# The mixer's mask and factor products on VectorE, and the first convolution tap on ScalarE

## The chip, the cores and the metric

The kernel runs on one core of one Trainium2 chip. The metric is the device time of the whole program in microseconds. Before the change three runs took 1018.86, 1017.07 and 1013.63 us; their median is 1017.07 us.

## The reference, cut to what matters

A token block of 256 rows and 1024 columns passes through two layers with attention-like mixers and MLPs, then through a hybrid mixer, and then through 16 experts chosen by a router. The change lies in the hybrid mixer's gated delta rule:

```python
qkv = jax.nn.silu(causal_depthwise_conv(qkv, conv_w)).astype(f32)   # 4 taps
q, k, v = jnp.split(qkv, 3, axis=-1)
q = l2_normalize(to_heads(q)) * (DN_HEAD_DIM ** -0.5)
k = l2_normalize(to_heads(k))
...
# gated_delta_rule, in chunks of 64 tokens, 8 heads of 128
diff = g_cum[..., :, None] - g_cum[..., None, :]
decay = jnp.where(causal, jnp.exp(jnp.where(causal, diff, 0.0)), 0.0)
a_mat = jnp.where(strict, jnp.einsum("bnhtk,bnhsk->bnhts", k_beta, k) * decay, 0.0) + jnp.eye(DN_CHUNK)
u = solve(a_mat, v_beta)
w = solve(a_mat, k_beta * jnp.exp(g_cum)[..., None])
qk = jnp.einsum("bnhtk,bnhsk->bnhts", q, k) * decay
...
def step(state, inp):
    v_new = u_c - jnp.einsum("bhtk,bhkv->bhtv", w_c, state)
    out = jnp.einsum("bhtk,bhkv->bhtv", q_c, state) + jnp.einsum("bhts,bhsv->bhtv", qk_c, v_new)
    state = state * gl_c[..., None, None] + jnp.einsum("bhsk,bhsv->bhkv", k_c, v_new)
```

Behind it stand a spatial gating unit, gates, an output projection, the router (top group, then two experts of it) and the experts.

## The kernel before

The program is written as calls on recorders, one for each engine (V for VectorE, S for ScalarE, G for GpSimd, PE, SP). Nothing is issued while it is recorded. A planner, the class Plan, gives each operation an estimated cost by engine and size (`_cost`, L163 to 192) and each hand-over between engines a price (a table at L30), and then decides in `order` the order on every engine, the place of every DMA on SP's queue, and the buffers: H is a pool of 47 blocks in SBUF, P the eight PSUM banks. Where it foresees TensorE idle it puts in filler matmuls of k_ones (L589). So an operation that changes its engine lets the planner order everything behind it anew. In the trace all recorded operations have line L594.

The stages in order are an attention layer, an MLP, a gated linear attention layer, an MLP, the hybrid mixer and the experts. In the trace the mixer begins at about 555 us. Its parts that matter here:

`qkv(hg)` (L1374), run for two groups of four heads. For q, k and v and for each pair of 128 features, projection matmuls fill one PSUM bank of banks 5 to 7 (H<-P,s_cw in the rows reads them as P); then the causal convolution goes over the bank in four taps: the first writes an accumulator (L1388), three more add to it shifted by one to three tokens (255, 254 and 253 elements in the rows). A tanh on ScalarE and a product on VectorE follow. There are 24 first taps, two to a bank.

`solve(hg, i)` (L1406), run for two head groups and two halves of the tokens, builds the chunk matrices, 128 x 256 each (four heads, two chunks of 64). E is an exponential of a matmul's result on ScalarE, masked with c_incl (L1430). From the squares of k and q come eight columns of factors (the tile hp; the power function runs on GpSimd). Ew is E times a factor (L1448), U is Ew times the product of keys (L1457), E is then scaled by another factor (L1458). kde, read from a PSUM bank with another factor, lets that bank go. L is a copy of U turned by matmuls, N its inverse in the making: five levels (L1478) each take L times a level mask, Lm (L1480), two sets of small matmuls, a copy on ScalarE and a subtraction on VectorE. The five Lm of a solve depend on L alone.

`recur(hg)` (L1499) then steps the state through the chunks. The mixer runs qkv(0), both solves of group 0 in turns, qkv(1), the first solve of group 1 together with recur(0), the second solve, and recur(1). The spatial gating unit's matmuls, 128 x 512, take their banks from 6 and 7 and are laid between.

VectorE also makes the "splits": `SCALAR_TENSOR_TENSOR H<-H,H 128x512 f16`, which write the low half of a weight or activation that goes into TensorE as two f16 parts.

Of the kernel before, what the change touches and what calls it, by code (L numbers as in the profile page):

```python
# [11 lines left out]
AF = mybir.ActivationFunctionType  # L12
OP = mybir.AluOpType
# [592 lines left out]
def block_kernel(ctx: ExitStack, tc: tile.TileContext, I: dict, out: bass.AP, dbg=None, stop=None):  # L606
    nc = tc.nc
    plan = Plan(nc)
    V, S, G, PE, SP = plan.DVE, plan.ACT, plan.POOL, plan.PE, plan.SP
# [13 lines left out]
    def PS(name, banks, dtype=F32):  # L623
        return plan.tile([128, 512 if dtype == F32 else 1024], name, dtype, "P", banks, psum=True)
# [4 lines left out]
    def A(shape, name, dtype=F32):  # L629
        return plan.tile(shape, name, dtype, "H", None)  # L630
# [4 lines left out]
    def B(shape, name, dtype=F32):  # L635
        return plan.tile(shape, name, dtype, "H", None)

    def C(shape, name, dtype=F32):
        return plan.tile(shape, name, dtype, "H", None)

    def sm(shape, name, dtype=F32, bufs=2):
        return plan.tile(shape, name, dtype, "s_" + name, bufs)
# [4 lines left out]
    def h4v(ap, n=4):  # L647
        return ap.rearrange("p (h t) -> p h t", h=n)

    def bc_free(col, n):  # L650
        return col[:, :, None].to_broadcast([col.shape[0], col.shape[1], n])

    def bc_mid(m, n):
        return m[:, None, :].to_broadcast([m.shape[0], n, m.shape[1]])
# [54 lines left out]
    def load_k8(src, c0, n, name):  # L709
        return [load_unit([(src[512 * u:512 * (u + 1), c0:c0 + n], 0)], 4, n, f"{name}{u}") for u in range(2)]  # L710
# [13 lines left out]
    def formB(po, us, c0, c1, xt, ts=slice(0, 256)):  # L724
        kt = 4 * len(us)
        for u, w in enumerate(us):
            for k in range(4):
                kk = 4 * u + k
                wh, wl = w.at(0, k, slice(c0, c1)), w.at(1, k, slice(c0, c1))
                xh, xl = tok(xt.h, kk, ts), tok(xt.l, kk, ts)  # L730
                o = like(po, xh)
                PE.matmul(o, wh, xh, start=(kk == 0), stop=False)
                PE.matmul(o, wh, xl, start=False, stop=False)
                PE.matmul(o, wl, xh, start=False, stop=(kk == kt - 1))
# [583 lines left out]
    def mixer(x, xt, then=None):  # L1318
# [8 lines left out]
        cw = sm([128, 96], "cw", bufs=1)  # L1327
# [46 lines left out]
        def qkv(hg):  # L1374
            res = []
            for r in range(3):
                us = load_k8(win, 1024 * r + 512 * hg, 512, f"d{r}")
                fT = A([128, 4, 256], f"dT{r}")
                for m in range(2):
                    p = PS("pqkv", (5, 6, 7))  # L1380
                    for mm in range(2):
                        c0 = 128 * (2 * m + mm)
                        formB(p[:, 256 * mm:256 * (mm + 1)], us, c0, c0 + 128, xt)
                    ac = C([128, 2, 256], "cacc")
                    for mm in range(2):
                        ft = 8 * r + 4 * hg + 2 * m + mm
                        pm = p[:, 256 * mm:256 * (mm + 1)]
                        V.tensor_scalar(ac[:, mm], pm, cw[:, 72 + ft:73 + ft], None, op0=OP.mult)  # L1388
                        for sh in range(1, 4):
                            tp = 24 * (3 - sh) + ft  # L1390
                            V.scalar_tensor_tensor(out=ac[:, mm, sh:], in0=pm[:, 0:256 - sh], scalar=cw[:, tp:tp + 1],
                                                   in1=ac[:, mm, sh:], op0=OP.mult, op1=OP.add)
                    th = C([128, 2, 256], "cth")
                    S.activation(th, ac, AF.Tanh, scale=0.5)
                    V.scalar_tensor_tensor(out=fT[:, 2 * m:2 * m + 2], in0=th, scalar=1.0, in1=ac, op0=OP.add, op1=OP.mult)
                res.append(fT)
            return res
# [8 lines left out]
        def solve(hg, i, qT, kT, vT):  # L1406
# [4 lines left out]
            def quads(p, lhs, rhs, width=64, c0=0):  # L1411
                for h4 in range(4):
                    for e in range(2):
                        PE.matmul(p[R[e], c0 + width * h4:c0 + width * (h4 + 1)], lhs[R[e], h4],
                                  rhs[R[e], h4] if len(rhs.shape) == 3 else rhs[R[e]], start=True, stop=True, skip_group_check=True)
# [11 lines left out]
            quads(p, gm, c_inclf)  # L1427
            E = B([128, 4, 64], "E")
            S.activation(E, h4v(p[:, 0:256]), AF.Exp)
            G.tensor_tensor(E, E, bc_mid(c_incl, 4), op=OP.mult)  # L1430
            yield
            w = sm([128, 10, 4], "hp", bufs=4)
            pt = {}
# [11 lines left out]
            V.tensor_tensor(w[:, 5], be[i][:, hs], rk, op=OP.mult)  # L1445
            V.tensor_tensor(w[:, 6], w[:, 5], rk, op=OP.mult)
            Ew = B([128, 4, 64], "Ew")
            G.tensor_tensor(Ew, E, bc_free(w[:, 6], 64), op=OP.mult)  # L1448
            V.tensor_tensor(w[:, 7], eg[i][:, 1, hs], rk, op=OP.mult)
            V.scalar_tensor_tensor(out=w[:, 4], in0=w[:, 1], scalar=0.5, in1=rk, op0=OP.mult, op1=OP.mult)  # L1450
            V.tensor_scalar(w[:, 8], eg[i][:, 0, hs], -1.0, None, op0=OP.mult)
# [3 lines left out]
            own(pk, kT, kT)  # L1455
            U = B([128, 4, 64], "U")
            V.tensor_tensor(U, h4v(pk[:, 0:256]), Ew, op=OP.mult)  # L1457
            G.tensor_tensor(E, E, bc_free(w[:, 3], 64), op=OP.mult)  # L1458
            pl = PS("pL", banks)
            quads(pl, U, c_id)  # L1460
            L = B([128, 4, 64], "L")
# [15 lines left out]
            yield  # L1477
            for lv in range(1, 6):  # L1478
                Lm = B([128, 4, 64], "Lm")
                G.tensor_tensor(Lm, L, bc_mid(lev[:, lv], 4), op=OP.mult)  # L1480
                pt_ = PS("pT", banks)
                quads(pt_, Lm, N)
                Tm = B([128, 4, 64], "Tm")
                S.activation(Tm, h4v(pt_[:, 0:256]), AF.Copy)
                pn = PS("pN", banks)
                quads(pn, NT, Tm)
                if lv < 5:
                    quads(pn, Tm, NT, c0=256)
                    V.tensor_tensor(NN.rearrange("p a h t -> p (a h t)"), NN.rearrange("p a h t -> p (a h t)"), pn, op=OP.subtract)
                else:  # L1490
                    V.tensor_tensor(N, N, h4v(pn[:, 0:256]), op=OP.subtract)
                yield
# [69 lines left out]

        z_gate(1)
        t0 = qkv(0)
        together(solve(0, 0, *t0), solve(0, 1, *t0))
        t1 = qkv(1)
        together(solve(1, 0, *t1), recur(0))
        together(solve(1, 1, *t1))
        together(recur(1))

# [78 lines left out]
        for c in range(2):  # L1649
            gated(tdn[c], "w_dn_out_2", c, oT, "wd")  # L1650
            for m in range(2):
# [5 lines left out]
                                       op0=OP.mult, op1=OP.subtract)  # L1657
# [462 lines left out]
```

## Time and profile before

| | us |
|---|---|
| median of three runs | 1017.07 |
| the profiled execution, own time | 1020.56 |
| its span, first to last instruction | 1018.9 |
| TensorE busy | 983.1 (96%) |
| VectorE busy | 810.9 (80%) |
| ScalarE busy | 582.2 (57%) |
| GpSimd busy | 78.5 (8%) |
| mean granted TensorE clock | 0.982 of full speed |

The profile gives busy times of each engine over the span or over a stretch, and lists of instructions with the idle time ahead of them and the engine that ended it. Instructions on one engine overlap by some tens of nanoseconds, so a group's busy time can be less than its count times its mean. A clock of 1.00 is 2.4 GHz, 0.50 is 1.2 GHz.

### The profile page before, as it was taken

What the parts mean: (1) busy time and instruction counts of PE and PEld (TensorE: products, weight loads), DVE (VectorE), ACT (ScalarE), POOL (GpSimd) and SP (SyncE); (2) the same over time, 40 slices, a digit from 0 to 9 for tenths busy, and PEclk for the clock granted to TensorE, in tenths of its full rate; (3) what the DMA queues carried; (4) which work ended last, traced back from release to release, by engine and by line L of the source; (5) the groups of instructions that cost most, each with busy time, mean ns of one, the idle gap of its engine ahead of it and who ended that gap; (6) DMA issues with size and microseconds to landing.
All of it is one profiled execution on the core that took longest, in us unless ns stands there. A gap on an engine that the chain in (4) does not pass through costs nothing. (4 is left out here: it accounts for less than half of the span.)

```text
span 1018.9 us, 22293 instructions
## 1 busy us (share of the span) xinstructions
PE 983.1 (96%) x8760; PEld 680.2 (67%) x8760; DVE 810.9 (80%) x1654; ACT 582.2 (57%) x1180; POOL 78.5 (8%) x121
## 2 busy tenths in 40 slices
PE   9999999999999999999999999989999999989994
PEld 8875777668458557766675787846788889553431
DVE  7899986656868898665659998958865688999985
ACT  7796555556448655555555752425543376568670
POOL 3000000000000000000001305003110000110000
PEclk9899999999999999999999999989899999999997
DMA  9927795676462467566867954414436676659992
GB/s 347 374 87 241 242 348 169 207 247 194 159 227 67 145 220 256 196 208 206 204 174 150 213 131 104 126 42 84 145 65 203 224 257 207 226 188 365 364 359 93
DMA packets 123009, 205.38 MB, mean 202 GB/s; under 512 B 7553, under 2 KB 43137, under 8 KB 122898
## 3 DMA queue, kind: packets, MB, share of 16 engines
q1 hardware_dynamic: 122898, 203.90, 64.7%
q8 instruction: 70, 1.15, 0.4%
q14 instruction: 41, 0.34, 0.1%
HBM read 202.82 MB, written 1.05 MB: 200 GB/s over the span
## 5 line engine op out<-in xcount | busy, mean ns | idle before, releaser
L594 PE MATMUL P<-H,H 128*128 128x256 f16 (+10 forms) x7736 | 918.8, 298 | 14.5 <-DVE H L594 6.7
L594 PEld LDWEIGHTS <-H 128*128 128x128 f16 (+3 forms) x6456 | 549.3, 99 | 261.6 <-issue 41.3
L594 ACT ACTIVATE H<-H 128x512 f16<-128x512 f32 (+2 forms) x777 | 443.9, 621 | 212.8 <-PE P L594 107.1
L594 DVE SCALAR_TENSOR_TENSOR H<-H,H 128x512 f16<-128x512 f32 (+2 forms) x715 | 456.4, 684 | 51.1 <-ACT H L594 48.9
L594 ACT ACTIVATE H<-P 128x256 f32<-128x256 f32 (+7 forms) x247 | 119.4, 497 | 190.3 <-PE P L594 181.2
L594 PEld LDWEIGHTS P<-H,H 64*64 64x64 f32 (+4 forms) x1424 | 67.7, 136 | 35.7 <-issue 23.0
L594 DVE TENSOR_TENSOR H<-H 128x512 f32<-128x512 f32 (+6 forms) x44 | 31.2, 709 | 44.2 <-ACT H L594 44.2
L594 POOL TENSOR_TENSOR s_bnr<-s_bnr,k_mhalf 128x1 f32<-128x1 f32 x14 | 13.4, 960 | 602.6 <-DVE s_bnr L594 602.6
L594 DVE SCALAR_TENSOR_TENSOR H<-P,H 128x512 f32<-128x512 f32 (+2 forms) x56 | 37.7, 684 | 20.0 <-PE P L594 11.7
L594 PE MATMUL P<-k_ident,H 128*128 128x128 f32 x256 | 46.1, 285 | 3.6 <-DVE H L594 2.6
L594 DVE TENSOR_TENSOR H<-H,H 128x512 f16<-128x512 f32 (+6 forms) x50 | 34.3, 694 | 10.2 <-ACT H L594 9.9
L594 PEld LDWEIGHTS P<-k_ident,H 128*128 128x128 f32 x256 | 31.9, 145 | 14.1 <-DVE H L594 5.6
L594 DVE TENSOR_TENSOR H<-H,P 128x512 f32<-128x512 f32 (+1 forms) x32 | 19.6, 613 | 13.7 <-PE P L594 13.6
L594 DVE SCALAR_TENSOR_TENSOR H<-P,s_cw,H 128x255 f32<-128x255 f32 (+2 forms) x72 | 29.7, 470 | 0.0
L594 DVE TENSOR_TENSOR H<-P,H 128x512 f16<-128x512 f32 (+2 forms) x38 | 23.5, 640 | 4.0 <-ACT H L594 4.0
L594 DVE SCALAR_TENSOR_TENSOR H<-H,s_bnr,H 128x512 f32<-128x512 f32 x28 | 21.2, 790 | 0.0
L594 DVE BATCH_NORM_STATS2 s_bns<-H 128x6 f32<-128x512 f32 x28 | 19.0, 683 | 1.8 <-ACT H L594 1.6
L594 DVE SCALAR_TENSOR_TENSOR H<-H,s_bnm,H 128x512 f32<-128x512 f32 x28 | 19.8, 741 | 0.0
L594 DVE SCALAR_TENSOR_TENSOR H<-H,P 128x512 f32<-128x512 f32 (+1 forms) x24 | 14.3, 594 | 6.0 <-ACT H L594 3.0
L594 PE MATMUL P<-H 128*64 128x64 f32 (+6 forms) x200 | 17.9, 255 | 0.7 <-DVE H L594 0.6
L589 PE MATMUL P<-k_ones 128*128 128x128 f16 x194 | 15.7, 235 | 1.1 <-DVE k_ones L594 1.1
L594 DVE TENSOR_TENSOR H<-P,s_hp 128x512 f32<-128x512 f32 (+1 forms) x16 | 10.9, 684 | 7.0 <-PE P L594 6.6
(220 smaller groups left out, 345.7 us busy)
## 6 DMA issues: line engine op xcount, KB each, us to landing
H<-in_mlp_w_dram SPq DMA_DIRECT2D x128, 512.0 KB, 4.9
H<-in_w_in_dram SPq DMA_DIRECT2D x64, 512.0 KB, 5.6
H<-in_expert_w_gate_dram SPq DMA_DIRECT2D x64, 256.0 KB, 5.9
H<-in_expert_w_up_dram SPq DMA_DIRECT2D x64, 256.0 KB, 5.9
H<-in_expert_w_down_dram SPq DMA_DIRECT2D x32, 512.0 KB, 7.0
H<-in_c_w_in_dram SPq DMA_DIRECT2D x24, 512.0 KB, 4.4
H<-in_a_w_in_dram SPq DMA_DIRECT2D x12, 512.0 KB, 8.1
H<-in_a_w_out_dram SPq DMA_DIRECT2D x8, 512.0 KB, 10.7
```

The costliest lines, as they stand in the source:

```text
L589: tc.nc.tensor.matmul(self.phys["P", ~i][:, 0:128], ap, ap, start=True, stop=True)
L594: fn(*[self._place(a) if isinstance(a, bass.AP) else a for a in args], **{k: self._place(a) if isinstance(a, bass.AP) else a for k, a in k ...
```

## The change

Four products of `solve` are given to VectorE instead of GpSimd: the causal mask of E, the factor products Ew and E, and the level masks Lm, 4 + 4 + 4 + 20 = 32 instructions of 128x256. The first tap of the convolution is given to ScalarE as a copy with a column as scale, instead of VectorE: 24 instructions of 128x256, read from PSUM.

```diff
-                        V.tensor_scalar(ac[:, mm], pm, cw[:, 72 + ft:73 + ft], None, op0=OP.mult)
+                        S.activation(ac[:, mm], pm, AF.Copy, scale=cw[:, 72 + ft:73 + ft])
...
-            G.tensor_tensor(E, E, bc_mid(c_incl, 4), op=OP.mult)
+            V.tensor_tensor(E, E, bc_mid(c_incl, 4), op=OP.mult)
...
-            G.tensor_tensor(Ew, E, bc_free(w[:, 6], 64), op=OP.mult)
+            V.tensor_tensor(Ew, E, bc_free(w[:, 6], 64), op=OP.mult)
...
-            G.tensor_tensor(E, E, bc_free(w[:, 3], 64), op=OP.mult)
+            V.tensor_tensor(E, E, bc_free(w[:, 3], 64), op=OP.mult)
...
-                G.tensor_tensor(Lm, L, bc_mid(lev[:, lv], 4), op=OP.mult)
+                V.tensor_tensor(Lm, L, bc_mid(lev[:, lv], 4), op=OP.mult)
```

The planner itself is unchanged, and up to the front of the mixer the order is the same on all engines. From there it differs. The number of real matmuls stays; the fillers go from 194 to 220.

First place, GpSimd and VectorE at the first head group's solves. The names: H are blocks, k_lev the level masks, P_115 bank 5 with a filled projection. GpSimd's rows before, from the first causal mask to the last level mask of the two solves:

```order
L594 TENSOR_TENSOR H_100<-H_100,k_c_incl_124 128x256 x2
L594 TENSOR_TENSOR s_hp_196<-s_hp_196,k_mhalf_137 128x8
L594 TENSOR_TENSOR H_89<-H_100,s_hp_196 128x256
L594 TENSOR_TENSOR H_100<-H_100,s_hp_196 128x256
L594 TENSOR_TENSOR s_hp_197<-s_hp_197,k_mhalf_137 128x8
L594 TENSOR_TENSOR H_89<-H_100,s_hp_197 128x256
L594 TENSOR_TENSOR H_100<-H_100,s_hp_197 128x256
L594 TENSOR_TENSOR H_109<-H_75,k_lev_132 128x256 x4
L594 TENSOR_TENSOR H_74<-H_75,k_lev_132 128x256 x4
L594 TENSOR_TENSOR H_83<-H_75,k_lev_132 128x256
L594 TENSOR_TENSOR H_75<-H_75,k_lev_132 128x256
```

VectorE after the change, the ten level masks and the taps on bank 5 behind them:

```order
L594 TENSOR_TENSOR H_109<-H_95,k_lev_132 128x256 x4
L594 TENSOR_TENSOR H_100<-H_100,P_113 128x256
L594 TENSOR_TENSOR H_74<-H_95,k_lev_132 128x256 x2
L594 TENSOR_TENSOR H_109<-H_95,k_lev_132 128x256
L594 TENSOR_TENSOR H_74<-H_95,k_lev_132 128x256
L594 TENSOR_TENSOR H_109<-H_95,k_lev_132 128x256
L594 TENSOR_TENSOR H_100<-H_100,P_111 128x256
L594 SCALAR_TENSOR_TENSOR H_105<-P_115,s_cw_163,H_105 128x255 x2
L594 TENSOR_TENSOR H_79<-H_95,k_lev_132 128x256
L594 SCALAR_TENSOR_TENSOR H_105<-P_115,s_cw_163,H_105 128x254 x2
L594 SCALAR_TENSOR_TENSOR H_105<-P_115,s_cw_163,H_105 128x253 x2
```

The masks have moved from GpSimd's queue to VectorE's, nine of them ahead of bank 5's accumulating taps. A little earlier on VectorE, Ew, E and U now stand ahead of kde, which stood ahead of U.

Second place, VectorE at the end of qkv(1): the last taps of the convolution, on bank 6 (P_116), which the spatial unit's matmuls use next. Before:

```order
L594 SCALAR_TENSOR_TENSOR H_103<-H_71,H_103 128x512 x2
L594 TENSOR_SCALAR H_83<-P_116,s_cw_163 128x256 x2
L594 SCALAR_TENSOR_TENSOR H_83<-P_116,s_cw_163,H_83 128x255 x2
L594 SCALAR_TENSOR_TENSOR H_83<-P_116,s_cw_163,H_83 128x254 x2
L594 TENSOR_TENSOR H_108<-H_108,P_113 128x512
L594 SCALAR_TENSOR_TENSOR H_83<-P_116,s_cw_163,H_83 128x253 x2
L594 TENSOR_TENSOR H_82<-P_117,k_m_full_134 128x512
```

After:

```order
L594 SCALAR_TENSOR_TENSOR H_86<-H_76,H_86 128x512
L594 SCALAR_TENSOR_TENSOR H_105<-P_116,s_cw_163,H_105 128x255 x2
L594 TENSOR_TENSOR H_95<-H_95,P_112 128x512
L594 SCALAR_TENSOR_TENSOR H_105<-P_116,s_cw_163,H_105 128x254 x2
L594 TENSOR_TENSOR H_67<-H_67,P_110 128x512
L594 SCALAR_TENSOR_TENSOR H_105<-P_116,s_cw_163,H_105 128x253 x2
L594 TENSOR_TENSOR H_109<-P_117,k_m_full_134 128x512
```

The pair of first taps is gone from VectorE, and two subtractions of the solves stand between the accumulating taps where one stood. ScalarE now makes the two first taps of a bank one behind the other, and VectorE's first accumulating tap waits for the second of them.

Third place, VectorE at the last factors (s_hp_199) of the first solves of group 1. Before:

```order
L594 TENSOR_TENSOR H_106<-k_c_id_123,H_106 128x256
L594 SCALAR_TENSOR_TENSOR H_79<-H_70,H_79 128x512 x2
L594 TENSOR_TENSOR s_hp_199<-s_db_168,s_hp_199 128x4
L594 TENSOR_TENSOR s_hp_199<-s_eg_178,s_hp_199 128x4
L594 SCALAR_TENSOR_TENSOR s_hp_199<-s_hp_199 128x4
L594 TENSOR_TENSOR s_hp_199<-s_hp_199 128x4
L594 TENSOR_SCALAR s_hp_199<-s_hp_199 128x4
```

After:

```order
L594 TENSOR_TENSOR H_89<-H_81,k_lev_132 128x256
L594 SCALAR_TENSOR_TENSOR H_108<-P_114,s_hp_197,H_108 64x128 x3
L594 TENSOR_TENSOR H_95<-H_100,P_113 128x512
L594 SCALAR_TENSOR_TENSOR H_108<-P_114,s_hp_197,H_108 64x128
L594 TENSOR_TENSOR H_103<-P_111,s_eg_178 64x512
L594 TENSOR_TENSOR H_100<-H_81,k_lev_132 128x256
L594 TENSOR_TENSOR H_108<-H_81,k_lev_132 128x256 x2
L594 SCALAR_TENSOR_TENSOR s_onm_222<-s_onm_222 128x4
L594 TENSOR_TENSOR s_hp_199<-s_db_168,s_hp_199 128x4
L594 TENSOR_SCALAR s_onm_222<-s_onm_222 128x4
L594 TENSOR_TENSOR s_hp_199<-s_eg_178,s_hp_199 128x4
```

Level masks (one more stands two rows above these) are now between and ahead of the factor steps, where before they stood on GpSimd.

On SP's queue two expert tiles, four DMAs of 256 KB, are issued ahead of the last projection weights of the mixer; three more expert units than before have been issued when the router's flag is made. In the router's chain on VectorE six splits of 128x512 now stand among the steps of the first token tile.

## Rows read from the trace of the kernel before

**Rows 1.** The page's first part: busy time, share of the span and instructions.

```profile
PE 983.1 (96%) x8760; PEld 680.2 (67%) x8760; DVE 810.9 (80%) x1654; ACT 582.2 (57%) x1180; POOL 78.5 (8%) x121
```

**Rows 2.** Stretches: us, busy of PE, PEld, DVE, ACT, POOL, clock, DMA share, GB/s.

```profile
560.00:600.00 40.00, 40.00 (x365) 31.36 (x363) 37.48 (x81) 24.55 (x46) 8.68 (x4) 1.00 0.79 185
600.00:620.00 20.00, 17.29 (x192) 14.59 (x190) 18.19 (x49) 9.18 (x42) 8.16 (x7) 0.94 0.79 160
620.00:640.00 20.00, 19.52 (x296) 16.57 (x294) 18.58 (x39) 7.62 (x15) 8.45 (x12) 0.98 0.14 45
640.00:660.00 20.00, 19.31 (x301) 16.38 (x300) 19.86 (x43) 8.49 (x17) 0.00 (x0) 1.00 0.42 131
660.00:680.00 20.00, 17.18 (x146) 9.04 (x141) 10.57 (x21) 5.06 (x9) 0.00 (x0) 0.83 0.17 56
...
700.00:720.00 20.00, 17.24 (x207) 13.87 (x207) 17.77 (x45) 9.35 (x27) 7.99 (x8) 1.00 0.28 65
720.00:740.00 20.00, 19.73 (x218) 15.40 (x219) 17.12 (x37) 10.94 (x25) 2.71 (x4) 0.83 0.57 171
```

**Rows 3.** Timeline of TensorE: start, us, instruction, count, [idle ahead, what ended it].

```profile
616.41 0.44 PE L594 MATMUL P<-k_ident,H 128*128 128x128 f32 x2 [1.27 <-DVE H L594]
617.26 0.51 PE L594 MATMUL P<-k_c_id,H 64*64 64x64 f32 x8 [0.42 <-DVE H L594]
...
666.24 2.29 PE L594 MATMUL P<-H,H 128*128 128x512 f16 x5 [2.25 <-DVE H L594]
...
707.65 1.60 PE L594 MATMUL P<-H,H 128*64 128x128 f32 x21 [1.39 <-DVE H L594]
...
719.87 2.74 PE L594 MATMUL P<-H,H 128*64 128x128 f32 x16 [1.37 <-DVE H L594]
```

**Rows 4.** VectorE's groups by form, 555 to 760 us: busy us, mean ns | idle.

```profile
L594 DVE TENSOR_SCALAR H<-P,s_cw 128x256 f32<-128x256 f32 x24 | 10.5, 474 | 0.2
...
L594 DVE TENSOR_TENSOR H<-k_c_id,H 128x256 f32<-128x256 f32 x8 | 4.4, 563 | 0.1
...
L594 DVE TENSOR_TENSOR H<-H,k_lev1t 128x256 f32<-128x256 f32 x4 | 1.7, 413 | 0.0
```

**Rows 5.** ScalarE's groups by form, 555 to 760 us.

```profile
L594 ACT ACTIVATE H<-P 128x256 f32<-128x256 f32 x24 | 8.6, 376 | 28.1 <-PE P L594 26.6 <-DVE s_hp L594 1.2
```

**Rows 6.** Timeline of VectorE at the end of qkv(1).

```profile
659.38 3.09 DVE L594 SCALAR_TENSOR_TENSOR H<-H,H 128x512 f16<-128x512 f32 x5
662.39 0.87 DVE L594 TENSOR_SCALAR H<-P,s_cw 128x256 f32<-128x256 f32 x2
```

**Rows 7.** GpSimd's groups by form, 555 to 760 us.

```profile
L594 POOL TENSOR_TENSOR H<-H,k_lev 128x256 f32<-128x256 f32 x20 | 14.1, 736 | 15.5 <-DVE H L594 13.5 <-ACT H L594 1.9
...
L594 POOL TENSOR_TENSOR H<-H,s_hp 128x256 f32<-128x256 f32 x8 | 5.1, 636 | 2.1 <-DVE s_hp L594 1.7
L594 POOL TENSOR_TENSOR H<-H,k_c_incl 128x256 f32<-128x256 f32 x4 | 3.4, 840 | 30.2 <-ACT H L594 30.1
```

**Rows 8.** Timelines of VectorE, then GpSimd, in the first chunk.

```profile
615.67 0.68 DVE L594 TENSOR_TENSOR H<-P,s_hp 128x512 f32<-128x512 f32 x1
...
616.80 0.41 DVE L594 TENSOR_TENSOR H<-P,H 128x256 f32<-128x256 f32 x1
617.13 0.67 DVE L594 TENSOR_TENSOR H<-P,s_hp 128x512 f32<-128x512 f32 x1
...
615.85 1.30 POOL L594 TENSOR_TENSOR H<-H,s_hp 128x256 f32<-128x256 f32 x2 [0.58 <-DVE s_hp L594]
```

**Rows 9.** Timelines of VectorE, then GpSimd, at the fourth chunk's factors.

```profile
704.11 0.62 DVE L594 TENSOR_TENSOR s_hp<-s_db,s_hp 128x4 f32<-128x4 f32 x1 [0.27 <-POOL s_hp L594]
704.66 0.15 DVE L594 TENSOR_TENSOR s_hp<-s_eg,s_hp 128x4 f32<-128x4 f32 x1
...
704.04 2.55 POOL L594 TENSOR_TENSOR H<-H,k_lev 128x256 f32<-128x256 f32 x4
```

**Rows 10.** One stretch of the experts, columns as in rows 2.

```profile
906.00:996.00 90.00, 85.68 (x796) 36.41 (x790) 82.50 (x153) 69.51 (x134) 0.00 (x0) 1.00 1.06 354
```

## The prediction

> **What bounds the kernel now.** I read the page's totals first [rows 1]: TensorE is busy 983.1 of 1018.9 us, VectorE 810.9, GpSimd 78.5. A kernel that is 96% TensorE can gain only where TensorE stands still or is clocked down, so the next view is the table of stretches [rows 2], kept to the mixer's chunk work, the only place that the change touches. Before 600 us TensorE is busy all 40.00 of 40.00 us: nothing is to be had there. Between 600 and 740 the six rows shown leave TensorE 2.71 + 0.48 + 0.69 + 2.82 + 2.76 + 0.27 = 9.7 us idle. The clock column is read with it: 0.94, 0.98, 0.83 and 0.83 of full speed in four of those rows, so 20 x (0.06 + 0.02 + 0.17 + 0.17) = 8.4 us are lost to the lower of the two levels (1.2 GHz instead of 2.4). All that an edit here can win is thus about 18 us, and only if every gap closes.
>
> Third view: who ended TensorE's gaps. The list of its matmuls [rows 3] shows four gaps over 1 us, all ended by VectorE: 1.27 us until 616.41 (and 0.42 until 617.26), 2.25 until 666.24, 1.39 until 707.65, 1.37 until 719.87. The clock falls behind the first, the second and the last, not behind 707.65. VectorE is the engine to watch: in 600 to 660 it is 18.2 to 19.9 us busy in each 20 [rows 2], while in 660 to 680 it works 10.57 us. So VectorE is nearly full up to about 667, and has room after.
>
> **Part 1, the taps.** Removed from VectorE: 24 first taps, 10.5 us [rows 4]. Added to ScalarE: 24 copies of 128x256 from PSUM with a column as scale. The nearest row is ScalarE's plain copy out of PSUM of the same shape, 376 ns [rows 5]: 24 x 0.376 = 9.0 us. ScalarE is busy 24.55 of the 40 us before 600 and 7.6 to 9.2 us of each 20 up to 640 [rows 2], so that work lies beside other work. From below, the two taps of a bank may overlap and cost less than 0.376 each; from above, a tap as long as VectorE's, 474 ns, gives 11.4 us. I take 9.0, the row of the same engine and shape.
>
> The bank's latency does not get shorter, however. Before, a bank was emptied by one engine: a pair of taps took 0.87 us, then the other taps followed at once [rows 6]. After, by the order, ScalarE makes both taps and VectorE's first accumulating tap waits for the second: 2 x 0.376 = 0.75 us plus a hop between engines, and ahead of it whatever ScalarE has in hand. So a bank is freed no earlier unless VectorE was the one that was late; where VectorE's queue is the delay, it is earlier by the 0.87 us that left the queue.
>
> A sentence of the Trainium skill speaks against this part: "ScalarE: Activation LUTs", section "What ACT_TABLE_LOAD costs", has a pointer operand (here the scale column) add about 93 ns to an activation; no row here shows one with such a scale on this shape. By it the taps would cost an estimated 24 x 0.093 = 2.2 us more of ScalarE's time, still beside other work.
>
> **Part 2, the 32 products.** GpSimd gives up 20 level masks, 14.1 us, 8 factor products, 5.1, and 4 causal masks, 3.4 [rows 7]: 22.6 us. VectorE takes 32 products of 128x256 with both operands in SBUF; its own of that kind takes 413 ns [rows 4], and the start of the next instruction comes 0.33 us after such a product (617.13 after 616.80 [rows 8]). So 32 x 0.33 to 32 x 0.413 = 10.6 to 13.2 us are added. That is about what the taps gave back.
>
> What also goes is interference. VectorE's subtraction from the identity has two SBUF operands as well and should cost 413 ns; it took 563 on average [rows 4], 8 x 0.15 = 1.2 us; GpSimd's masks run in the same stretches. At 704.11 a 128x4 step took 0.62 us, the next 0.15, while GpSimd made four masks from 704.04 on [rows 9]; there are three such slow steps within 2 us, 3 x 0.47 = 1.4 us, just ahead of the gap that ended at 707.65. So at least 2.6 us of VectorE time come back.
>
> VectorE's account up to 667: minus 10.5 for the taps, plus 16 products, 5.3 to 6.6, minus about 1: **5 to 6 us lighter**, in the stretch where it is full. After 667: plus 5.3 to 6.6, minus 1.6: **4 to 5 us heavier**, where it idles more than that.
>
> **Where it reaches TensorE.** (a) The first chunk, gap until 617.26. Before: factor on VectorE, then GpSimd makes Ew and E from 615.85 on, 1.30 us for two, then U on VectorE at 616.80 [rows 8]. After, Ew, E and U stand one behind another on VectorE: 615.85 and two steps of 0.33 put U at 616.5, 0.3 us earlier. But in the new order kde, which at 615.67 released TensorE's transposes at 616.41, stands behind U, about 1 us later. I count 0, bounds -0.7 and +1 us.
>
> (b) The gap of 2.25 us until 666.24. The first spatial matmul needs the bank that qkv(1)'s last taps empty; VectorE came to them at 662.39, after five splits, 3.09 us from 659.38 [rows 6]. In the new order the pair of taps is gone and VectorE has 5 to 6 us less behind it, but two subtractions of the solve now stand between the accumulating taps where one stood. I take **-2 us**: the gap shrinks to a few tenths. Bounds: 0 (TensorE feeds those taps itself, so its earlier end only moves the gap) and -2.25 and the whole 3.4 us of lost clock, -5.7.
>
> (c) The gap of 1.39 us until 707.65. The slowed steps, 1.4 us, go. Five level masks now stand on VectorE just ahead of the same steps, 5 x 0.33 = 1.7 us. I take **-0.5**, since some of them fall into idle time; bounds -1.4 and +1.7.
>
> (d) 719.87: VectorE's own splits ended that gap; no term, bounds -1.4 and +1.4.
>
> (e) The clock. I let half of one of the two drops of 3.4 us go: **-1.5**, bounds -6.8 and +3.4.
>
> (f) The tail. From 906 to 996 the DMA share is 1.06 at 354 GB/s [rows 10]: the expert weights set the end. In the new order three more 0.26-MB units are issued before the router's flag, 3 x 0.26 MB / 354 GB/s = 2.2 us off; against that, six weight splits of 0.62 us (3.09 / 5 [rows 6]) now stand in the router's chain on VectorE for the first tokens, 3.7 us on. They are missing later, so I take **+0.5**, bounds -2.2 and +3.7.
>
> Sum: 0 - 2 - 0.5 + 0 - 1.5 + 0.5 = **-3.5 us**, so 1017.1 us by the profiled execution (1020.6). That one lay 3.5 us above the median of the three runs (1017.1), so the forecast is 1017.1 - 3.5 = **1013.6 us**.
>
> **Rivals.** *VectorE was the whole cause.* With 5 to 6 us less in its queue up to 667, the gaps at 616 and 666 close (1.69 and 2.25 us) with their clock, 1.6 + 3.4: -8.9, and with the 1.4 at 707 -10.3: about **1007 us**, down to 1002 if 719.87 and its 3.4 go too. For it: all four gaps end on VectorE [rows 3]. Against it: the solve is a chain of small steps through TensorE, ScalarE and VectorE, and of the moved products only the causal mask and Ew stand in it, since the level masks are made ahead of their use.
>
> *Nothing reaches TensorE.* 96% busy, the masks were off its path, the gain at 666 appears again at the next hand-over: **1017 us**, 1015 to 1020. For it: TensorE is full before 600, and GpSimd's slowness nowhere ended a gap of TensorE directly [rows 3].
>
> *The masks block the bank (slower).* In the new order ten level masks of the first two chunks stand almost together on VectorE, 10 x 0.33 = 3.3 us, ahead of the accumulating taps on bank 5; before, GpSimd made them beside it, 10 x 0.7 = 7 us [rows 7]. If TensorE has less than about 2 us of other work at that place, a gap over 1.3 us opens, of the size that brought the lower clock behind three of four gaps: up to 3.3 + 3.4 = 6.7 us, **1023.8 us**. It decides from the point where bank 6 and bank 7 are full too. A rule of the Trainium skill makes this sharper ("PSUM — Partial Sum Buffer", section "PSUM bank collisions raise a hardware error"): two engines may not read one bank at once. By it ScalarE's taps can't run beside VectorE's, so the bank waits for both engines in turn; the order shows that wait, the trace of before none.
>
> **How the numbers follow.** Chances: forecast 0.42 (own range 1010 to 1018), whole cause 0.22, nothing 0.18, masks block 0.18. The measurement tells 0.5%, 5.1 us, from no change, so the bounds are 1012.0 and 1022.2. Faster: 0.20 of the second and 0.16 of the forecast's lower end, 0.36. Slower: 0.16 of the last. Same: 0.48. The range runs from the middle of the second case to the last one's value: 1004 to 1024, leaving out about 0.1 below and 0.1 above.
>
> **What would show it.** Right: VectorE's busy time in 600 to 667 falls by 4 to 7 us; the gap at the first spatial matmul is under 0.6 us; the identity subtraction falls to about 415 ns; ScalarE's tap costs 0.35 to 0.5 us; TensorE's busy time is unchanged and no new gap over 1.3 us appears between 600 and 760. Wrong: a gap over 1.3 us at bank 5's taps, with the clock at half behind it; the gap at the first spatial matmul still 2 us, with VectorE idle before it; or the end set by the router's chain, seen as expert weights landing later against the router's flag.

## The result and the profile after

The changed kernel takes 1012.30 us, the median of nine runs (1010.94 to 1013.66), against 1017.07 for nine runs of the kernel before. The ratio is 0.9947, with a 95% interval of 0.9933 to 0.9961: 0.5% faster, 4.8 us by the medians. The forecast was 1013.6.

| | before | after |
|---|---|---|
| median of nine runs, us | 1017.07 | 1012.30 |
| the profiled execution, own time, us | 1020.56 | 1011.38 |
| its span, us | 1018.9 | 1009.6 |
| its mean granted TensorE clock | 0.982 | 0.988 |

The page's first part after the change, which answers to [rows 1]:

```profile
PE 977.2 (97%) x8786; PEld 679.7 (67%) x8786; DVE 804.2 (80%) x1662; ACT 591.9 (59%) x1204; POOL 55.5 (5%) x89
```

GpSimd lost 23 us of work and ScalarE gained 10, which is about what the moved instructions take. VectorE is 6.7 us lighter in sum. The stretches, which answer to [rows 2] (us, busy of PE, PEld, DVE, ACT and POOL, clock, DMA share, GB/s), and the same two stretches up to and behind the mixer's first spatial matmul:

```profile
600.00:620.00 20.00, 18.03 (x246) 15.59 (x244) 16.20 (x50) 9.55 (x44) 3.29 (x2) 1.00 0.69 173
620.00:640.00 20.00, 20.00 (x312) 17.13 (x311) 17.02 (x41) 6.87 (x15) 0.00 (x0) 1.00 0.08 26
640.00:660.00 20.00, 19.12 (x316) 16.44 (x314) 19.29 (x38) 12.64 (x27) 0.00 (x0) 1.00 0.25 75
660.00:680.00 20.00, 19.76 (x181) 11.87 (x182) 9.41 (x19) 9.94 (x25) 0.93 (x1) 1.00 0.27 88
...
700.00:720.00 20.00, 19.70 (x252) 16.08 (x251) 19.54 (x46) 11.64 (x25) 1.97 (x2) 1.00 0.68 151
720.00:740.00 20.00, 17.85 (x273) 15.26 (x271) 14.40 (x31) 9.69 (x20) 0.00 (x0) 0.91 0.37 107
...
600.00:667.00 67.00, 63.98 (x929) 53.01 (x927) 55.57 (x132) 31.66 (x89) 3.29 (x2) 1.00 0.36 100
667.00:760.00 93.00, 90.14 (x1092) 69.18 (x1090) 74.04 (x171) 49.29 (x123) 8.02 (x6) 0.98 0.32 86
```

The two last stretches in the kernel before:

```profile
600.00:667.00 67.00, 60.36 (x859) 50.82 (x857) 63.64 (x142) 27.46 (x78) 16.61 (x18) 0.96 0.46 117
667.00:760.00 93.00, 89.65 (x966) 64.42 (x965) 65.18 (x141) 43.76 (x112) 19.27 (x22) 0.94 0.33 81
```

TensorE's idle time from 600 to 760 us is 160 less its busy time: 9.99 us before, 5.88 after. That sum is used for every experiment below. VectorE is 8.1 us lighter up to 667 and 8.9 heavier behind it.

The gaps of TensorE that are left, answering to [rows 3] (start, us, instruction, count, [idle ahead, what ended it]):

```profile
610.02 0.66 PE L594 MATMUL P<-k_ident,H 128*128 128x128 f32 x4 [1.47 <-ACT H L594]
...
613.62 0.56 PE L594 MATMUL P<-k_c_id,H 64*64 64x64 f32 x12 [0.22 <-DVE H L594]
...
658.79 0.68 PE L594 MATMUL P<-H,H 64*64 64x64 f32 x16 [0.73 <-DVE H L594]
...
660.16 0.45 PE L594 MATMUL P<-H,H 64*64 64x64 f32 x8 [0.31 <-DVE H L594]
...
704.47 1.75 PE L594 MATMUL P<-H,H 128*64 128x128 f32 x15 [0.21 <-DVE H L594]
...
727.21 0.68 PE L594 MATMUL P<-H,H 64*64 64x64 f32 x16 [2.15 <-DVE H L594]
```

Why the two profiled executions differ by 9.2 us and the medians by 4.8: the runs of one kernel do not all get the same clock. In a series of 30 runs of the kernel before, the mean clock lay between 0.982 and 0.991 with a median of 0.988, and the time between 1022.2 and 1014.1. The profiled execution of before had 0.982, as low as the lowest of them. The nine runs after had 0.985 to 0.989, median 0.987. So the clock's 8.4 us that [rows 2] shows lost were mostly that one execution's bad luck, and the medians hold no such part. Over all runs of this study a thousandth of clock goes with about 0.7 us; at one clock of 0.988 that makes, from the means of the 30 and of the nine runs, an estimated 1017.0 us before and 1011.7 after.

In the profiled pair, from the start of VectorE's first accumulating tap to its first step on the router's logits the time fell from 304.95 to 294.90 us (-10.05: about 4.1 of idle time and 6.6 of clock, less 0.45 of added fillers). From there to the start of VectorE's last instruction it rose from 129.24 to 131.71 us (+2.5), and the first accumulating tap came 1.8 us earlier, about 1.0 of which arose in work that the change leaves alone.

### The profile page after: what moved, and what is told of

It reads as the page before. It is cut to its first block, busy times and chain, and to the rows that moved or that the text cites. A ratio compares the mean times of both kernels' runs of the same rounds, so it can differ in the third digit from the quotient of the medians.

```text
span 1009.6 us, 22338 instructions
## 1 busy us (share of the span) xinstructions
PE 977.2 (97%) x8786; PEld 679.7 (67%) x8786; DVE 804.2 (80%) x1662; ACT 591.9 (59%) x1204; POOL 55.5 (5%) x89
## 5 line engine op out<-in xcount | busy, mean ns | idle before, releaser
L594 PE MATMUL P<-H,H 128*128 128x256 f16 (+8 forms) x7780 | 914.7, 297 | 10.4 <-DVE H L594 6.0
L594 PEld LDWEIGHTS <-H 128*128 128x128 f16 (+2 forms) x6456 | 547.5, 99 | 255.8 <-issue 35.9
L594 PEld LDWEIGHTS P<-H,H 64*64 64x64 f32 (+4 forms) x1472 | 70.1, 138 | 33.2 <-issue 18.8
L589 PE MATMUL P<-k_ones 128*128 128x128 f16 x220 | 18.9, 247 | 2.6 <-ACT H L594 1.5
L589 PEld LDWEIGHTS <-k_ones 128*128 128x128 f16 x220 | 16.5, 114 | 2.7 <-issue 1.3
```

Source lines behind the costliest of these rows:

```text
L589: tc.nc.tensor.matmul(self.phys["P", ~i][:, 0:128], ap, ap, start=True, stop=True)
L594: fn(*[self._place(a) if isinstance(a, bass.AP) else a for a in args], **{k: self._place(a) if isinstance(a, bass.AP) else a for k, a in k ...
```

## The experiments

The planner orders everything behind a change of engine anew, so an edit changes two things at once: which engine does the work, and the order on all engines. The first eight experiments take these apart. `plan.add` names the engine for which the planner reckons and places an operation, and separately the function that is issued. With the two set apart, TensorE's and SP's orders stay row for row those of one kernel, while the engines are those of another.

**Both parts, in the order of before.**

```diff
-                        V.tensor_scalar(ac[:, mm], pm, cw[:, 72 + ft:73 + ft], None, op0=OP.mult)
+                        plan.add("DVE", "tensor_scalar", nc.scalar.activation, (ac[:, mm], pm, AF.Copy), dict(scale=cw[:, 72 + ft:73 + ft]))
...
-                G.tensor_tensor(Lm, L, bc_mid(lev[:, lv], 4), op=OP.mult)
+                plan.add("POOL", "tensor_tensor", nc.vector.tensor_tensor, (Lm, L, bc_mid(lev[:, lv], 4)), dict(op=OP.mult))
...
```

The other three products are edited like Lm.

> The planner plans as for the kernel before (taps costed and placed as VectorE's, products as GpSimd's), so TensorE's and SP's orders are those of before, row by row; only the engine that executes the taps (ScalarE) and the 32 products (VectorE) is that of the changed kernel. Theory A, the engines did it (VectorE's queue is lighter up to 667 us, and GpSimd's interference is gone): 1012 to 1014 us, and the identity subtraction falls to about 420 ns. Theory B, the new order did it: 1017 us or above, since the old order now has products in places that were planned for GpSimd.

Measured: 1023.62 us, ratio 1.0058 (1.0037 to 1.0079). The very engines of the changed kernel make the program 0.6% slower in the old order. VectorE's accumulating taps show a part of the reason (group by form, 555 to 765 us: busy, mean ns | idle ahead, releaser):

```profile
L594 DVE SCALAR_TENSOR_TENSOR H<-P,s_cw,H 128x255 f32<-128x255 f32 x24 | 10.6, 477 | 10.8 <-ACT H L594 10.8
...
L594 DVE TENSOR_TENSOR H<-k_c_id,H 128x256 f32<-128x256 f32 x8 | 3.3, 420 | 0.1
```

VectorE waits 10.8 us for ScalarE's first taps. At the end of qkv(1) one sees it happen (ScalarE, then VectorE, then TensorE):

```profile
667.67 0.47 ACT L594 ACTIVATE H<-P,s_cw 128x256 f32<-128x256 f32 x1
...
668.17 1.65 DVE L594 SCALAR_TENSOR_TENSOR H<-P,s_cw,H 128x255 f32<-128x255 f32 x4 [1.61 <-ACT H L594]
...
671.26 2.27 PE L594 MATMUL P<-H,H 128*128 128x512 f16 x7 [3.17 <-DVE H L594]
```

ScalarE reaches the second tap behind other work of its own queue, VectorE stands 1.61 us, and the first spatial matmul's gap is 3.17 us instead of 2.25. The identity subtraction is at 420 ns, so the interference with GpSimd is gone here too, and yet the kernel is slower.

**Both parts undone, in the order of after.** The mirror image: planned as S and V, issued on VectorE and GpSimd.

```diff
-                        S.activation(ac[:, mm], pm, AF.Copy, scale=cw[:, 72 + ft:73 + ft])
+                        plan.add("ACT", "activation", nc.vector.tensor_scalar, (ac[:, mm], pm, cw[:, 72 + ft:73 + ft], None), dict(op0=OP.mult))
...
-                V.tensor_tensor(Lm, L, bc_mid(lev[:, lv], 4), op=OP.mult)
+                plan.add("DVE", "tensor_tensor", nc.gpsimd.tensor_tensor, (Lm, L, bc_mid(lev[:, lv], 4)), dict(op=OP.mult))
...
```

> The mirror image: planned as the changed kernel, with its orders of TensorE and SP, but the taps run on VectorE and the 32 products on GpSimd, as before the change. Theory A: 1016 to 1019 us, with the identity subtraction back above 500 ns and VectorE's gaps ahead of TensorE back. Theory B: 1012 to 1013 us.

Measured: 1019.76 us, ratio 1.0010 (0.9996 to 1.0025). The new order by itself is worth nothing. TensorE's largest gap lies in the first chunk:

```profile
612.83 1.12 PE L594 MATMUL P<-k_ident,H 128*128 128x128 f32 x4 [3.74 <-ACT H L594]
```

At 606.80 in this run VectorE still had the last bank's two taps ahead of their accumulation (0.86 us), so the tanh behind them began on ScalarE at 610.09, and the squares, for which TensorE's transposes wait, came behind that tanh. So neither theory held: the engines alone lose 0.6%, the order alone gives 0, both together win 0.5%.

**Each part alone, in the order of before.** The tap's line of the first diff alone, then the products' lines alone.

> TensorE's and SP's orders of the kernel before, products on GpSimd as before; only the 24 first taps run on ScalarE, in the places that were planned for VectorE. Theory A (engine speed) would have this faster than before, 1014 us. Theory C, drawn from the first four runs: in the old order ScalarE reaches a tap late, behind a tanh that waits for VectorE, so VectorE waits for taps (10.8 us of waiting in the run with both parts); the loss of that run, about 5 us at equal clock, is the taps': 1020 to 1023 us.

> TensorE's and SP's orders of the kernel before, taps on VectorE as before; only the 32 products run on VectorE, in the places planned for GpSimd. Theory C: VectorE is some 5 us heavier up to 667 us but the interference of about 1 us goes there and 1.6 us later: within 2 us of before, 1016 to 1019 us. If the loss of the run with both parts came from the products in places not planned for them: 1020 to 1023 us.

Measured: tap alone 1020.81 us, 1.0027 (1.0013 to 1.0042); products alone 1020.09 us, 1.0024 (1.0010 to 1.0038). The tap's loss is the wait named above; VectorE's first accumulating taps of this run:

```profile
L594 DVE SCALAR_TENSOR_TENSOR H<-P,s_cw,H 128x255 f32<-128x255 f32 x24 | 10.5, 477 | 11.5 <-ACT H L594 11.5
```

The losses add up to about that of both, 0.3 + 0.2 against 0.6%. I had put all of it on the taps; nearly half of it is the products'. With them alone on VectorE TensorE's three gaps in the first chunk are 1.70 + 1.28 + 1.02 us, where they were 1.03 + 1.27 + 0.42; that VectorE's longer queue is the reason there is inferred, not shown.

**Each part undone alone, in the order of after.** The tap's line of the second diff alone, then the products' lines alone.

> TensorE's and SP's orders of the changed kernel, its products on VectorE; only the taps are back on VectorE, in the places planned for ScalarE. VectorE then carries both, 10.5 us more up to 667 us. Theory C: the gaps of 3.7 us in the first chunk and 2.6 us at the first spatial matmul, which the run with both parts undone showed, are the taps': 1016 to 1019 us. If the products made the gain: 1012 to 1013 us.

> TensorE's and SP's orders of the changed kernel, its taps on ScalarE; only the 32 products are back on GpSimd. Theory C: the interference comes back (the identity subtraction near 490 ns or above) and the products' 0.65 to 0.85 us replace 0.42, 2 to 3 us of which reach TensorE: 1013 to 1015 us. If the products made the gain: 1016 to 1018 us.

Measured: with the taps back on VectorE 1023.23 us, 1.0059 (1.0038 to 1.0079); with the products back on GpSimd **1012.25 us, 0.9943 (0.9923 to 0.9963)**, the same as the changed kernel. Both lie outside what I expected of theory C, 1016 to 1019 and 1013 to 1015 us. The second is the run that settles the most. In the new order the tap is everything: it is worth 0.7% where the products are on GpSimd (1.0010 to 0.9943), and 1.1% where they are on VectorE (1.0059 to 0.9947). Part of both is a lower clock, a median of 0.981 in the run with the taps back and 0.9835 in the one with both parts back; by the means, at one clock of 0.988 and 0.7 us for a thousandth, the tap is worth an estimated 5.5 and 7.3 us. That lower clock is not the luck of single executions: all seven with the taps back got 0.980 to 0.983, while 25 of the kernel before, timed beside them, got 0.983 to 0.990. So part of the clock belongs to the kernel and not to the execution; what in the kernel sets it, these runs do not show.

The products' change of engine is worth nothing that these runs resolve (intervals of about 2 us to either side), though the interference is back. The identity subtraction (VectorE by form, 555 to 765 us), first after the change, then with the products back on GpSimd:

```profile
L594 DVE TENSOR_TENSOR H<-k_c_id,H 128x256 f32<-128x256 f32 x8 | 3.4, 421 | 0.0
```

```profile
L594 DVE TENSOR_TENSOR H<-k_c_id,H 128x256 f32<-128x256 f32 x8 | 4.0, 499 | 0.1
```

563 ns before [rows 4], 421 after, 499 with the masks on GpSimd again: the interference is real, and in this order it does not show in the time. The Trainium skill states the cause ("SBUF — State Buffer", section "Who interferes with whom"): a VectorE instruction with two inputs in SBUF shares a read port with GpSimd's reads. The trace agrees, 563 and 499 ns against 421. The page's first part for the run with the products back shows what it all weighs:

```profile
PE 976.6 (97%) x8786; PEld 679.8 (67%) x8786; DVE 796.3 (79%) x1630; ACT 592.0 (59%) x1204; POOL 76.3 (8%) x121
```

VectorE is busy 796.3 us there and 804.2 in the changed kernel. The 32 products cost it 12.4 us (below), so about 4.5 us of interference were saved in return, and 7.9 us more is what the move leaves on VectorE.

**Each part alone, planned anew.** The tap's line or the products' lines of the change itself.

> Only the first tap goes to ScalarE; the products stay on GpSimd; planned anew. Theory A gives the larger part of the gain to the taps, since they take 10.5 us from VectorE up to 667 us: 1013 to 1015 us. A rival, that the products and the interference are the cause: 1017 us. If the new order alone decides, anything between 1010 and 1020.

> Only the 32 products go to VectorE; the taps stay there too; planned anew. Theory A: VectorE is 5 to 6 us heavier up to 667 us and only some 1 us of interference comes back there, so the gap ahead of the first spatial matmul grows: 1018 to 1021 us. The rival, that the interference and GpSimd's slowness were the cause: 1012 to 1014 us.

Measured: tap alone 1015.34 us, 0.9974 (0.9957 to 0.9992); products alone 1017.71 us, 1.0007 (0.9988 to 1.0026). As expected the tap carries a gain and the products none, though both times lie just outside the ranges given, 1013 to 1015 and 1018 to 1021 us. But the run with the tap alone has exactly the engines of the run with the products back, at 1012.25 us: 3 us lie between two orders of the same work. In the slower of the two, TensorE's largest gap, and VectorE in front of it:

```profile
653.65 5.50 DVE L594 SCALAR_TENSOR_TENSOR H<-H,H 128x512 f16<-128x512 f32 x9
659.40 1.26 DVE L594 SCALAR_TENSOR_TENSOR H<-P,s_cw,H 128x255 f32<-128x255 f32 x3 [0.24 <-ACT H L594]
660.58 0.68 DVE L594 TENSOR_TENSOR H<-H,P 128x512 f32<-128x512 f32 x1
...
661.40 1.12 PE L594 MATMUL P<-H,H 64*64 64x64 f32 x16 [2.71 <-DVE H L594]
```

Nine splits, 5.50 us, stand on VectorE ahead of a solve's subtraction (660.58) for which TensorE waits 2.71 us. The changed kernel has eight splits at that place, 5.00 us, but from 652.31 us on, and its gap there is 0.73. The gap that the changed kernel has left, 2.15 us until 727.21, is of the same kind, with six splits in front:

```profile
722.60 3.70 DVE L594 SCALAR_TENSOR_TENSOR H<-H,H 128x512 f16<-128x512 f32 x6
726.21 0.35 DVE L594 SCALAR_TENSOR_TENSOR H<-H,s_onm,H 128x128 f32<-128x128 f32 x1
726.47 0.69 DVE L594 TENSOR_TENSOR H<-H,P 128x512 f32<-128x512 f32 x1
```

**Other orders by other prices.** The last four change a price in the planner, and so the order, of four sets of engines. The line behind an operation sets its estimated cost, here that of the tap:

```diff
                         S.activation(ac[:, mm], pm, AF.Copy, scale=cw[:, 72 + ft:73 + ft])
+                        plan.ops[-1] = plan.ops[-1][:4] + (465.0,) + plan.ops[-1][5:]
```

The products on GpSimd get 736.0 in the same way. First the engines of before, then tap on ScalarE with the products on GpSimd at the new price:

> The engines of the kernel before, all of them; only the price that the planner has for the 32 products on GpSimd is changed, from 658 to 736 ns, the mean that the trace of before shows for the level masks. It shows what a new order alone does with unchanged engines. Theory C (the engines matter only through the order that is planned for them, and orders differ by chance): anywhere within 5 us of before, 1012 to 1022 us. If the planner's wrong price was what held the old order back: 1013 us or less.

> Taps on ScalarE, products on GpSimd, planned anew with the products at 736 instead of 658 ns. These are the engines of the run with the tap alone (1015.3 us) and of the run in the changed kernel's order with the products back (1012.3 us). If the tap's gain is robust against the order: 1012 to 1016 us. If it is an accident of one order: anything up to 1020 us.

Then the changed kernel with the tap at its measured price, and tap and products on GpSimd with both prices:

> The changed kernel with one price of the planner put right: the tap on ScalarE at 465 ns, as the trace after the change shows it, instead of 265. Engines as in the changed kernel. If the fit of the plan to the engines is what counts, VectorE's waits for the tap (2.1 us) shrink: 1010 to 1012 us. If orders scatter by chance: 1010 to 1018 us.

> Taps on ScalarE at the price of 465 ns, products on GpSimd at 736 ns: both prices as the traces show them, the products left where they were before the change. If the products' move is worth nothing and the price of the tap counts: 1010 to 1013 us, as fast as the changed kernel or faster. If orders scatter by chance: 1010 to 1018 us.

Measured: engines of before 1020.67 us, 1.0027 (1.0009 to 1.0045); tap with a new price for the products 1015.39, 0.9969 (0.9952 to 0.9987); tap with both prices 1016.12, 0.9986 (0.9971 to 1.0002); and the changed kernel with the tap's price put right **1009.13, 0.9920 (0.9894 to 0.9946)**, the fastest of all. Its largest gap of TensorE between 600 and 760 us is 0.55 us:

```profile
600.00:667.00 67.00, 65.99 (x935) 53.80 (x933) 53.86 (x126) 29.21 (x84) 3.30 (x2) 1.00 0.37 104
667.00:760.00 93.00, 90.91 (x1090) 69.75 (x1089) 68.90 (x161) 44.65 (x115) 8.85 (x6) 1.00 0.32 86
```

```profile
L594 DVE SCALAR_TENSOR_TENSOR H<-P,s_cw,H 128x255 f32<-128x255 f32 x24 | 10.5, 476 | 1.1 <-ACT H L594 0.9
```

VectorE's wait for taps fell to 1.1 us from the 2.1 of the changed kernel, and TensorE's idle time to 3.1 us. The same group in the changed kernel:

```profile
L594 DVE SCALAR_TENSOR_TENSOR H<-P,s_cw,H 128x255 f32<-128x255 f32 x24 | 10.5, 480 | 2.1 <-ACT H L594 2.1
```

A truer price did not always help, however. The products' price put right made the engines of before 3.6 us slower, where 1013 us or less was expected if the wrong price had held the old order back; with the tap on ScalarE it changed nothing (1015.34 to 1015.39 us); and the tap's price put right beside it changed nothing for the better (1015.39 to 1016.12), where 1010 to 1013 was expected if that price counted. Only with the products on VectorE did it gain 3 us. So these four runs do not tell a better fit from orders that scatter by some microseconds. All runs side by side, with that idle time (160 us less TensorE's busy time in the two stretches); each experiment's ratio is to runs of the kernel before timed in its own series, whose medians were 1017.26, 1017.38 and 1017.13 us:

| taps on | products on | order | idle, us | median, us | ratio |
|---|---|---|---|---|---|
| VectorE | GpSimd | own (before) | 9.99 | 1017.07 | 1 |
| VectorE | GpSimd | own, products' price 736 | 11.2 | 1020.67 | 1.0027 |
| VectorE | GpSimd | of after | 9.8 | 1019.76 | 1.0010 |
| VectorE | VectorE | own | 10.5 | 1017.71 | 1.0007 |
| VectorE | VectorE | of before | 12.7 | 1020.09 | 1.0024 |
| VectorE | VectorE | of after | 11.2 | 1023.23 | 1.0059 |
| ScalarE | GpSimd | own | 8.6 | 1015.34 | 0.9974 |
| ScalarE | GpSimd | own, products' price 736 | 7.0 | 1015.39 | 0.9969 |
| ScalarE | GpSimd | own, both prices | 8.2 | 1016.12 | 0.9986 |
| ScalarE | GpSimd | of before | 13.5 | 1020.81 | 1.0027 |
| ScalarE | GpSimd | of after | 5.4 | 1012.25 | 0.9943 |
| ScalarE | VectorE | own (after) | 5.9 | 1012.30 | 0.9947 |
| ScalarE | VectorE | own, tap's price 465 | 3.1 | 1009.13 | 0.9920 |
| ScalarE | VectorE | of before | 14.7 | 1023.62 | 1.0058 |

Eight of these kernels are issued on the engines that they were planned for. The five with the tap on ScalarE took 1009.1 to 1016.1 us, the three with the tap on VectorE 1017.1 to 1020.7; if the orders drew their times at random, that split would come up once in 56. Of the six issued on other engines than planned, only the one with the tap on ScalarE in the order of after is faster than before. The time follows TensorE's idle time in the mixer roughly; the run with only the taps back in the order of after, 1023.23 us at 11.2, stands out by its clock.

## Why the prediction was right or wrong, point by point

**What bounds the kernel.** Right: TensorE's busy time before 600 us stayed full, and the gain lies in the idle time of the mixer, 9.99 to 5.88 us. Wrong about the clock: all 8.4 us were read as something that the edit could win. Most of them belonged to the one execution profiled, whose clock of 0.982 is among the lowest of its kernel. Term (e), -1.5 us, stood on that; in the medians of the clock, 0.988 and 0.987, there is nothing.

**What the account left out.** It follows the moved work through one order: VectorE gets lighter, so the gaps close. In the old order the moved work alone loses 0.6%; the gain needs the order that the planner made for the new engines. So the number, 1013.6 against 1012.30 us, came nearer than the account deserves: term (e) is not there, term (f) is 2 us too small, and small gaps without a term, about -1.6 us, made up for part of that.

**Part 1.** The direction was right, and the tap is the cause, in an order planned for it: undone alone in the new order it costs all of the gain and more. The duration was mis-sized. The nearest row was 376 ns, and the tap takes 465 (ScalarE by form, 553 to 760 us, after the change):

```profile
L594 ACT ACTIVATE H<-P,s_cw 128x256 f32<-128x256 f32 x24 | 9.9, 465 | 5.2 <-DVE H L594 2.7 <-PE P L594 2.4
...
L594 ACT ACTIVATE H<-P 128x256 f32<-128x256 f32 x27 | 10.1, 382 | 20.7 <-PE P L594 18.8 <-DVE H L594 1.6
```

The tap is inside the stated 0.35 to 0.5 us, and 465 less 382 is 83 ns for the scale column. With the 93 ns that the Trainium skill gives for a pointer operand ("ScalarE: Activation LUTs", section "What ACT_TABLE_LOAD costs") the estimate would have been 0.376 + 0.093 = 0.469 us; the trace agrees, 0.465. Since the instructions of a pair overlap, the sum came out at 9.9 us against 9.0. The hop that the text named is there; VectorE waited 2.1 us for taps after the change and 10.8 in the old order, so its price goes with where ScalarE's queue has the tap.

**Part 2.** The sums held: 7.4 + 3.4 + 1.6 = 12.4 us of products on VectorE, forecast 10.6 to 13.2:

```profile
L594 DVE TENSOR_TENSOR H<-H,k_lev 128x256 f32<-128x256 f32 x20 | 7.4, 424 | 0.0
...
L594 DVE TENSOR_TENSOR H<-H,s_hp 128x256 f32<-128x256 f32 x8 | 3.4, 420 | 0.0
...
L594 DVE TENSOR_TENSOR H<-H,k_c_incl 128x256 f32<-128x256 f32 x4 | 1.6, 421 | 0.5 <-ACT H L594 0.5
```

The identity subtraction fell to 421 ns, forecast 415. The interference was put at 2.6 us at least; by the two runs in one order it is about 4.5. But the step from there to TensorE failed: the products' engine is worth nothing in the new order (1012.25 against 1012.30 us), although the interference is back.

**VectorE's account** was forecast at 5 to 6 us lighter up to 667 and 4 to 5 heavier behind it; from 600 on it was 8.1 and 8.9. The sign held, but not for the reason given. Only 6.6 us of the taps lie between 600 and 667 (the others come before 600), and 16 products, 3.6 + 1.7 + 0.8 = 6.1 us, came in their place; with some 1 us of interference gone the edit itself makes that stretch about 1.5 us lighter. Most of the rest is 12 splits that the new order put elsewhere, ten of them behind 667. VectorE by form, 600 to 667 us, before and then after:

```profile
L594 DVE SCALAR_TENSOR_TENSOR H<-H,H 128x512 f16<-128x512 f32 x32 | 20.7, 682 | 0.3
...
L594 DVE TENSOR_SCALAR H<-P,s_cw 128x256 f32<-128x256 f32 x15 | 6.6, 474 | 0.0
```

```profile
L594 DVE SCALAR_TENSOR_TENSOR H<-H,H 128x512 f16<-128x512 f32 x20 | 13.1, 688 | 0.7 <-ACT H L594 0.7
```

The account was made as if the order were fixed.

**Where it reaches TensorE.** (a) 0 was forecast for the first chunk; the three gaps until 617.26, of which the forecast named two, went from 1.03 + 1.27 + 0.42 to 1.47 + 0.22 + 0.28, -0.75 us, just past the lower bound of -0.7. (b) -2 us was forecast ahead of the spatial unit's first matmul; 2.25 became 0.73 + 0.31 in two gaps, and five fillers, 0.45 us, stand between them: about -1.2, in the right place and too large. (c) -0.5 was forecast, 1.39 became 0.21: -1.2. The end of the interference, named as the reason, is not needed for that: with the products back on GpSimd TensorE is busy 20.00 of 20.00 us from 700 to 720. (d) No term; 1.37 us at 719.87 went and 2.15 at 727.21 came, +0.8, within the bounds. Together these four are -2.3 us against the forecast's -2.5. Smaller gaps at 630.15, 648.87 and 662.85, 0.48, 0.59 and 0.51 us, which had no term, are gone too, and make up most of the rest of the 4.1 us. (f) +0.5 was forecast for the tail and it measured +2.5 in the profiled pair, inside the stated bounds; that the six splits in the router's chain cost more than the three earlier units won would fit, but no run parts the two. All four kernels in the order of before have 129.2 to 129.9 us there, all four in the order of after 131.7 to 133.4, so this belongs to the order.

**The signs.** The identity subtraction, the tap's cost and the gap ahead of the first spatial matmul (0.31 us, until 660.16) came out as named. TensorE's busy time, which was to stay, fell by 5.9 us; that goes with the higher clock of the execution. Two signs failed: VectorE's busy time from 600 to 667 fell by 8.1 us instead of 4 to 7, and two gaps over 1.3 us stand where none was to appear, 1.47 us until 610.02 (1.03 before) and 2.15 until 727.21.

**The rivals.** *VectorE was the whole cause* gave 1007 us; the changed kernel does not reach that. One better order, the tap's price put right, came to 1009.1 with the gaps all but closed, so the figure for closed gaps was about right. *Nothing reaches TensorE* is out. *The masks block the bank* is out: with ten masks standing on VectorE, TensorE was busy 20.00 of 20.00 us from 620 to 640. What lay outside all of them is the rival that the order decides: with the same engines the time went from 1012.3 to 1020.8 us by the order alone.

**What stays open.** Why an order planned with the products on VectorE is better even when GpSimd executes them (1012.25 against 1015.3, 1015.4 and 1016.1 us for three orders planned with them on GpSimd) is not settled. That the planner then believes masks earlier to be had, while the chip has slack for them, was argued only. Two orders planned with the products on VectorE and the tap on ScalarE were timed, too few to exclude chance. Whether the tap's price put right gained its 3 us by a better fit or by chance is open too.

## What to carry to other kernels

Where a planner writes the order, an engine move is two edits, and the way to tell them apart is to plan for one engine and issue on another; here the engines alone lost 0.6%, the order alone nothing, and both together gained 0.5%. Here the move paid where the receiving engine's queue had the operation early enough: VectorE waited 10.8 us for taps in the order that lost and 2.1 in the one that won. The planner's price for the moved operation belongs to the change, and other prices are a cheap way to other orders; the tap's put from 265 to its measured 465 ns gained another 3 us, while the other corrected prices gained nothing, so each order has to be timed. Before a clock drop in a profile is counted as something to win, the clocks of the other runs of the same kernel should be looked at.

## What the runs showed of the hardware

- One program got mean clocks from 0.982 to 0.991 in 30 runs, and its time went with it, 1022.2 to 1014.1 us; about 0.7 us for a thousandth.
- A ScalarE copy of 128x256 out of PSUM took 382 ns, and 465 with a column as scale.
- VectorE's subtraction of 128x256 with two SBUF operands took 421 ns, and 563 or 499 on average where GpSimd made masks beside it. By the two runs in one order GpSimd's 32 products cost VectorE about 4.5 us in all, and the kernel nothing that these runs resolve.
